# A down-projection written as 44 steps in a fixed order, with reordered first loads and longer distances in the delta rule

## The chip, the cores and the metric

The kernel runs on one core of one Trainium2 chip. The metric is device time in microseconds of one launch. The core's engines, as the profile names them, are TensorE (PE for its matmuls, PEld for its weight loads), VectorE (DVE), ScalarE (ACT), GpSimd (POOL) and SyncE (SP). Each runs its own instructions strictly in order and waits on semaphores of the others. Loads and stores are issued from the queue of one of them: weights from SP, hidden tiles and residual tiles of the down-projection from POOL.

## The reference

One layer over 512 positions of width 2048, in float32. `mem` has 256 tokens, the feed-forward width is 5632.

```python
h = rmsnorm(x, mix_norm)
proj = h @ w_mix_in
y_gdn = gdn_group(proj, ...)         # 8 heads x 128: conv, silu, l2norm, gated delta rule, rmsnorm, gate
y_sc = shortconv_group(proj, ...)    # 1024 channels: gated causal conv of width 3
x = x + concatenate([y_gdn, y_sc]) @ w_mix_out
h = rmsnorm(x, xattn_norm)
mem_n = rmsnorm(mem, mem_norm)
x = x + memory_xattn(h, mem_n, w_xq, w_xk, w_xv, w_xo)
h = rmsnorm(x, ffn_norm)
u = causal_dwconv(h @ w_ffn_up, ffn_conv)
gate, up = u[..., :5632], u[..., 5632:]
x = x + (silu(gate) * up) @ w_ffn_down
return rmsnorm(x, final_norm)
```

In the gated delta rule each head solves, per chunk, a unit triangular system (I + A) with A from the products of its keys, and carries a 128 x 128 state over the chunks; its output goes through an rmsnorm of its own.

## The kernel before

Activations stand transposed: channels on the 128 partitions, the 512 positions along the free axis, so one tile of 128 x 512 holds 128 channels. Matrix products keep float32 accuracy by splitting each operand into a rounded part and a rest (`split` for activations, `wpiece` for weights: ACT makes the rounded part `hi`, DVE subtracts it from the original for `lo`) and by three matmuls for each tile pair (`mm3`: hi times hi, hi times lo, lo times hi). A weight piece is 128 x 1024; it has five buffers for the raw load (`wst`) and three each for `whi` and `wlo`.

The stages in order, by the time at which PE works on them: the key projection of the memory and the two products that follow it (`psk`, `pswk`, to about 304 us), the product of the value side with the output weights (`psmo`, to 404), the q, k, v and z projections of the eight heads (to 851) and the short convolution's (`pssc`, to 1135), the mixer's output (`psx`, to 1309), attention (to 1490), the up-projection (to 2386.6), and the down-projection `psd`, whose last steps run in two halves with the final norm (to 3059.9).

Most code is put in order by a scheduler of the framework. A block under `tc.manual_schedule(engines=...)` keeps the order in which it is written on the engines that it names.

**Down-projection.** Four groups `gq` of four output tiles, each with its PSUM bank (`bank`, eight banks in two pools of five and three, so two groups find room). In a group, 11 steps `c` each bring four hidden tiles (`hid_parts`: load from DRAM on POOL's queue, then `split` into `hdh` and `hdl`) and two weight pieces, for 2 x 2 x 4 x 3 = 48 matmuls of 128 x 512. After a group, each output tile gets the residual tile `x2_d` added (load on POOL, addition on DVE, L865) and its squares summed (`add_squares`: ACT squares, POOL adds to `acc3`, L239; the very first tile's square is written by ACT without an addition). The last group has 10 steps here, no squares at its end, and its eleventh step is the tail in two halves of 256 positions.

**Delta rule.** `delta` is a generator for one head. `weave` and `tick` insert its pieces among the matmuls of the projections: each `yield a, b` ends a piece, adds `a` to a clock that counts PE work, and asks that the next piece come `b` units later. Three matmuls of a projection count 0.65.

**First loads.** The column table `cols` (all norm and convolution weights) is loaded whole on SP, the eight double tiles of `mem` on ACT's queue, and weights follow on SP. `mem_proj` multiplies by `w_xk`, two output tiles in one bank, the first wholly before the second; after the first pair, `mem_norm` sums the squares of `mem` on POOL and multiplies them with `ones` on PE (L230).

Of the kernel before, what the change touches and what calls it, by code (L numbers as in the profile page):

```python
# [25 lines left out]
FC = 4  # L26
EPS = 1e-6
NEG = -1.0e30
B = 32
# [38 lines left out]
def trunk(ctx: ExitStack, tc: tile.TileContext, g):  # L68
# [47 lines left out]
    nc.vector.memset(ones, 1.0)  # L116

# [10 lines left out]
    hgain = cpool.tile([P, 1], F32, tag="hgain", name="hgain")  # L128
    nc.vector.tensor_scalar(hgain, col(C_GAIN), 0.5, None, op0=ALU.mult)

    def wpiece(src):

        st = wp.tile([P, 1024], F32, tag="wst", name=nm("wst"), bufs=5)
# [7 lines left out]
        nc.scalar.copy(hi, st)  # L141
        nc.vector.tensor_tensor(lo, st, f(hi), op=ALU.subtract)  # L142
        return hi, lo
# [99 lines left out]
    mws, m2s = [], []  # L243
    early = {}
    for i in range(KT // 2):
        m2 = T("mem")
        nc.scalar.dma_start(m2.rearrange("p (k m) -> p k m", k=2), g["mem"][2 * i : 2 * i + 2].rearrange("k p m -> p k m"))
        m2s.append(m2)
    with tc.manual_schedule(engines={mybir.EngineType.Activation, mybir.EngineType.DVE, mybir.EngineType.SP}):
        for i in range(KT // 2):  # L250
            if i in (0, 2):
                early[0, i // 2] = wpiece(g["w_xk"][0, i // 2])
            mh, ml = T("mwh", F32R), T("mwl", F32R)
            for k in range(2):
                sl = slice(k * NMEM, (k + 1) * NMEM)
                c = col(C_MEMN + 2 * i + k)
                nc.scalar.activation(mh[:, sl], m2s[i][:, sl], AF.Identity, scale=c)
                nc.vector.scalar_tensor_tensor(ml[:, sl], m2s[i][:, sl], c, f(mh)[:, sl], op0=ALU.mult, op1=ALU.subtract)
                mws.append((mh[:, sl], ml[:, sl]))
# [3 lines left out]
    def mem_norm():  # L263
        for i in range(KT // 2):
            add_squares(macc, m2s[i], i == 0)
# [4 lines left out]
    def mem_proj(w, then=None):  # L270

        out = []
        for n2 in range(KT // 2):
            ps = PM("psk")
            for q in range(2):
                first = [early[0, i] for i in range(2)] if then and n2 == 0 and q == 0 else None
                proj(lambda i: w[2 * n2 + q, i], mws, ps[:, q * NMEM : (q + 1) * NMEM], ready=first)
            if then and n2 == 0:
                then()
            t = T("kt")  # L280
            nc.vector.tensor_tensor(t.rearrange("p (q m) -> p q m", q=2), ps.rearrange("p (q m) -> p q m", q=2), rmem, op=ALU.mult)
            th, tl = T("kth", F32R), T("ktl", F32R)
            nc.scalar.copy(th, t)
            nc.vector.tensor_tensor(tl, t, f(th), op=ALU.subtract)
            for q in range(2):
                out.append((th[:, q * NMEM : (q + 1) * NMEM], tl[:, q * NMEM : (q + 1) * NMEM]))
        return out

    kts = mem_proj(g["w_xk"], mem_norm)
    nc.sync.dma_start(mk, g["masks"])  # L290
    ident = mk[:, M_ID, :]
    idb = cpool.tile([P, CB, B], F32, tag="idb", name="idb")
    nc.sync.dma_start(idb, g["idb"])
# [137 lines left out]
    def delta(h, q, k, v, z):  # L431
# [18 lines left out]
        yield 0.5, 0  # L450
# [13 lines left out]

        psk = PG("pskk")
        four(psk, lambda j: k4[:, j], lambda j: k4[:, j])
        yield 0.9, 0
# [5 lines left out]
        nc.vector.tensor_tensor(dt, psq, dt, op=ALU.mult)  # L473
        at = dt
        yield 0.9, 0
        psv = PG("psvt")
        for j in range(4):
            nc.tensor.transpose(v4(psv)[:, j], v4_[:, j], ident)
        nc.vector.tensor_tensor(v4(v), v4(psv), bc(nk, P), op=ALU.mult)
        yield 0.5, 2.5  # L480
# [31 lines left out]
        yield 0, 9.0  # L512
# [5 lines left out]
        yield 0.5, 1.2  # L518

        for s in (32, 64):  # L520
# [7 lines left out]
            yield 0.5, 1.2  # L528
# [11 lines left out]
            yield 0.7, 1.5  # L540
# [33 lines left out]
        yield 0, 3.0  # L574
        psn = PG("psn")
        nc.tensor.matmul(psn, ones, s1, start=True, stop=True)
# [6 lines left out]
        yield 0.9, 0  # L583
# [168 lines left out]
    def raw(src):  # L752
        t = wp.tile([P, 1024], F32, tag="wst", name=nm("wst"), bufs=5)
# [10 lines left out]
    def sums(s, i):  # L764

        if i == 0:
            return wp.tile([P, 1024], F32, tag="wst", name=nm(s), bufs=5)
# [68 lines left out]
    def hid_parts(c):  # L836
        out = []
        for k in range(FC):
            t = T("hid")
            nc.gpsimd.dma_start(t, hid_d[c * FC + k])  # L840
            out.append(split(t, "hd"))
        return out

# [3 lines left out]
    for gq in range(KT // GN):  # L847
        last = gq == KT // GN - 1
        pss = [bank(gq, q) for q in range(GN)]
        nc_ = NC_ - 1 if last else NC_  # L850
        for c in range(nc_):
            hid = hid_parts(c)
            for n2 in range(GN // 2):
                hi, lo = wpiece(g["w_dn"][c, gq * GN // 2 + n2])
# [105 lines left out]
```

## Time and profile before

| | |
|---|---|
| median of 3 runs | 3063.89 us (3062.74 to 3080.56) |
| the profiled execution | 3061.85 us, span 3059.9 us |
| granted TensorE clock, mean | 0.978 |
| PE busy | 2874.5 us, 94% |
| DVE busy | 1815.5 us, 59% |
| ACT busy | 1339.3 us, 44% |
| POOL busy | 358.4 us, 12% |
| mean DMA rate | 155 GB/s |

Busy time is an average over stages with different limits, so the reading goes by stretches. In a row of a group, the figures after the bar are the busy time and the mean duration of one instruction, then the idle time of that engine just before them and what ended it. In the timeline, a row is a start, a duration and the instruction, with the idle time before it in brackets. A name such as `psd<-hdh,whi` is output from inputs: here the bank of the down-projection from a rounded hidden tile and a rounded weight piece. Matmuls overlap, so their durations don't add up; the distance between starts is what counts. Numbers of the whole program that the page gives are of this one execution.

### The profile page before, as it was taken

How to read it: one execution, taken by the hardware profiler on the slowest of the kernel's cores; microseconds unless marked ns; L12 is line 12 of the kernel's file. 1: busy time of each engine (PE TensorE's matmuls, PEld its weight loads, DVE VectorE, ACT ScalarE, POOL GpSimd, SP SyncE). 2: the span in 40 equal slices, each digit the busy share in tenths (PEclk: the TensorE clock that was granted, in tenths of full speed). 3: DMA queues.
4: the chain of work that ended last, by engine and by line, in shares of the span. 5: the costliest groups of instructions: out<-in, count | busy, mean ns of one | idle time of the engine just before them, and what ended most of it. 6: DMA issues, size and time to landing. Idle time of an engine off the chain costs nothing.

```text
span 3059.9 us, 44141 instructions
## 1 busy us (share of the span) xinstructions
PE 2874.5 (94%) x17521; PEld 2531.8 (83%) x17521; DVE 1815.5 (59%) x2680; ACT 1339.3 (44%) x1879; POOL 358.4 (12%) x438
## 2 busy tenths in 40 slices
PE   7999999999999999999999999999999887878785
PEld 7999788777778888888899999999999665656564
DVE  5445747767753344456788888888888433333334
ACT  5564643443432232245655555555555323323222
POOL 1120000110100001101200000000000203021211
PEclk9999999999999999999999999999999999989898
DMA  6685753333232234455666666666666635354451
GB/s 208 230 287 183 248 156 100 101 84 95 84 100 93 97 127 148 145 180 177 178 175 180 167 170 162 174 179 167 168 164 169 210 111 196 106 173 140 149 162 55
DMA packets 178799, 473.96 MB, mean 155 GB/s; under 512 B 26512, under 2 KB 50464, under 8 KB 178592
## 3 DMA queue, kind: packets, MB, share of 16 engines
q1 hardware_dynamic: 128576, 333.74, 33.0%
q0 software_dynamic: 29984, 102.80, 14.9%
q10 hardware_dynamic: 20032, 34.61, 3.1%
q8 instruction: 137, 2.24, 0.3%
q14 instruction: 70, 0.57, 0.1%
HBM read 427.02 MB, written 44.06 MB: 154 GB/s over the span
## 4 chain that ended last, share of the span: by engine, by line
PE 58%; issue 5%; DVE 3%; ACT 2%; DMA 2%; POOL 1%; DVEq 0%; ACTq 0%; SPq 0%; POOLq 0%
PE px L778 5%; PE px L776 5%; PE px L777 5%; PE psd L153 4%; PE psd L154 4%; PE psd L152 3%; PE pz L776 3%; PE pz L778 3%; PE pz L777 3%; PE pssc L152 3%; PE pssc L154 3%; PE pssc L153 3%; PE psx L153 2%; PE psx L154 2%; PE psx L152 2%
## 5 line engine op out<-in xcount | busy, mean ns | idle before, releaser
L142 DVE TENSOR_TENSOR wlo<-wst,whi 128x1024 fp32r<-128x1024 f32 x408 | 497.7, 1229 | 734.8 <-ACT whi L141 720.8
L141 ACT CAST whi<-wst 128x1024 fp32r<-128x1024 f32 x408 | 424.0, 1049 | 971.2 <-PE psd L153 396.8
L760 ACT CAST whi<-wst 128x1024 fp32r<-128x1024 f32 x176 | 184.5, 1048 | 290.8 <-PE px L777 143.7
L153 PE MATMUL psd<-hdl,whi 128*128 128x512 f32 (+1 forms) x720 | 293.3, 409 | 15.4 <-DVE hdl L148 15.4
L776 PE MATMUL px<-xoh,whi 128*128 128x256 f32 x1056 | 299.6, 284 | 3.6 <-ACT whi L760 3.2
L778 PE MATMUL px<-xoh,wlo 128*128 128x256 f32 x1056 | 299.4, 283 | 0.0
L777 PE MATMUL px<-xol,whi 128*128 128x256 f32 x1056 | 299.3, 283 | 0.0
L152 PE MATMUL psd<-hdh,whi 128*128 128x512 f32 (+1 forms) x720 | 205.4, 399 | 98.6 <-ACT hdh L147 98.5
L154 PE MATMUL psd<-hdh,wlo 128*128 128x512 f32 (+1 forms) x720 | 285.4, 397 | 0.0
L761 DVE TENSOR_TENSOR wlo<-wst,whi 128x1024 fp32r<-128x1024 f32 x176 | 215.3, 1223 | 96.8 <-ACT whi L760 52.0
L152 PEld LDWEIGHTS psd<-hdh,whi 128*128 128x128 f32 x720 | 134.7, 192 | 143.0 <-ACT hdh L147 117.6
L776 PEld LDWEIGHTS px<-xoh,whi 128*128 128x128 f32 x1056 | 203.3, 192 | 4.0 <-ACT whi L760 3.4
L778 PEld LDWEIGHTS px<-xoh,wlo 128*128 128x128 f32 x1056 | 203.4, 193 | 0.0
L777 PEld LDWEIGHTS px<-xol,whi 128*128 128x128 f32 x1056 | 203.3, 193 | 0.0
L778 PE MATMUL pz<-xoh,wlo 128*128 128x256 f32 x704 | 199.3, 283 | 0.9 <-DVE wlo L761 0.9
L776 PE MATMUL pz<-xoh,whi 128*128 128x256 f32 x704 | 199.5, 283 | 0.4 <-ACT whi L760 0.4
L777 PE MATMUL pz<-xol,whi 128*128 128x256 f32 x704 | 199.4, 283 | 0.0
L153 PEld LDWEIGHTS psd<-hdl,whi 128*128 128x128 f32 x720 | 141.9, 197 | 62.6 <-DVE hdl L148 34.8
L760 ACT CAST whi<-s 128x1024 fp32r<-128x1024 f32 x132 | 138.1, 1048 | 86.2 <-PE px L777 60.8
L154 PEld LDWEIGHTS psd<-hdh,wlo 128*128 128x128 f32 x720 | 141.9, 197 | 27.7
L761 DVE TENSOR_TENSOR wlo<-s,whi 128x1024 fp32r<-128x1024 f32 x132 | 161.2, 1223 | 0.6 <-ACT whi L760 0.6
L152 PE MATMUL psq<-hh,whi 128*128 128x512 f32 x384 | 157.8, 411 | 0.0
(306 smaller groups left out, 7363.8 us busy)
## 6 DMA issues: line engine op xcount, KB each, us to landing
wst<-in_w_up SPq DMA_DIRECT2D x132, 512.0 KB, 4.8
wst<-in_w_mix SPq DMA_DIRECT2D x112, 512.0 KB, 3.5
s<-in_w_up POOLq DMA_DIRECT2D x88, 512.0 KB, 6.4
wst<-in_w_dn SPq DMA_DIRECT2D x88, 512.0 KB, 4.3
hid<-hid_d POOLq DMA_DIRECT2D x176, 256.0 KB, 4.2
s<-in_w_up SPq DMA_DIRECT2D x44, 512.0 KB, 4.9
wst<-in_w_xk SPq DMA_DIRECT2D x32, 512.0 KB, 3.5
wst<-in_w_xq SPq DMA_DIRECT2D x32, 512.0 KB, 4.5
```

Source lines behind the costliest of these rows:

```text
L141: nc.scalar.copy(hi, st)
L142: nc.vector.tensor_tensor(lo, st, f(hi), op=ALU.subtract)
L152: nc.tensor.matmul(ps, wh, xh, start=first, stop=False)
L153: nc.tensor.matmul(ps, wh, xl, start=False, stop=False)
L154: nc.tensor.matmul(ps, wl, xh, start=False, stop=last)
L760: nc.scalar.copy(hi, t)
L761: nc.vector.tensor_tensor(lo, t, f(hi), op=ALU.subtract)
L776: nc.tensor.matmul(ps, hi[:, c], xh, start=first and k == 0, stop=False, skip_group_check=True)
L777: nc.tensor.matmul(ps, hi[:, c], xl, start=False, stop=False, skip_group_check=True)
L778: nc.tensor.matmul(ps, lo[:, c], xh, start=False, stop=k == HK - 1, skip_group_check=True)
```

## The change

The down-projection is written as a list of 44 steps (group and `c`). Loads of hidden tiles are asked for two steps ahead, and the parts of hidden tiles and of weight pieces are made two steps and two pieces ahead, on ACT, DVE and POOL in the order written. PE's matmuls of a step stand piece by piece and bank by bank. The tail's parts are made in the same way.

At the start, `cols` is loaded in two portions; the `mem` tiles and four weight pieces come on SP in one written order; the first two output tiles of `mem_proj` are taken together, and the squares of `mem` are used by the norm only after the third pair of output tiles. In `delta`, the products of keys with keys and the transposes are grouped differently, the distances are longer, and the head's norm uses a split operand and two matmuls with rounded ones (`onesr`) where it used one in float32.

```diff
@@ the first loads
-    nc.sync.dma_start(cols, g["cols"])
+    nc.sync.dma_start(cols[:, :C_FFNN], g["cols"][:, :C_FFNN])
...
+        load_mem(0)
+        e0 = raw_piece(g["w_xk"][0, 0])
+        e1 = raw_piece(g["w_xk"][1, 0])
+        for i in (1, 2, 3):
+            load_mem(i)
+        e2 = raw_piece(g["w_xk"][0, 1])
+        e3 = raw_piece(g["w_xk"][1, 1])
+        for i in (4, 5, 6, 7):
+            load_mem(i)
+        nc.sync.dma_start(cols[:, C_FFNN:], g["cols"][:, C_FFNN:])
+        early[0, 0] = parts(e0)
+        mem_parts(0)
+        early[1, 0] = parts(e1)
...
+            if begin and n2 == 0:
+                ps = [PG("psk")[:, :NMEM] for _ in range(2)]
+                for i in range(2):
+                    for k in range(8):
+                        for q in range(2):
+                            hi, lo = early[q, i]
+                            mm3(ps[q], hi[:, k * P : (k + 1) * P], lo[:, k * P : (k + 1) * P], *mws[8 * i + k], i == 0 and k == 0, i == 1 and k == 7)
+                for i in range(1, KT // 2):
+                    add_squares(macc, m2s[i], False)
...
+            if begin and n2 < 2:
+                continue
+            if begin and n2 == 2:
+                mem_norm()
@@ def delta
-        yield 0.5, 0
+        psk = PG("pskk")
+        four(psk, lambda j: k4[:, j], lambda j: k4[:, j])
+        yield 1.4, 1.0
...
-        yield 0, 9.0
+        yield 0, 12.5
...
-        yield 0.5, 1.2
+        yield 0.5, 4.5
...
-            yield 0.5, 1.2
+            yield 0.5, 2.8
...
-            yield 0.7, 1.5
+            yield 0.7, 2.8
...
-        yield 0, 3.0
+        sh, sl = split(s1, "sn")
+        yield 0, 6.0
         psn = PG("psn")
-        nc.tensor.matmul(psn, ones, s1, start=True, stop=True)
+        nc.tensor.matmul(psn, onesr, sh, start=True, stop=False)
+        nc.tensor.matmul(psn, onesr, sl, start=False, stop=True)
@@ the down-projection
+    steps = [(gq, c) for gq in range(KT // GN) for c in range(NC_)]
+    raws, parts_, ws = {}, {}, {}
+
+    def hid_load(i):
+        if i < len(steps):
+            raws[i] = [T("hid") for _ in range(FC)]
+            for k in range(FC):
+                nc.gpsimd.dma_start(raws[i][k], hid_d[steps[i][1] * FC + k])
+
+    def hid_split(i, k):
+        if i < len(steps):
+            parts_.setdefault(i, []).append(split(raws[i][k], "hd"))
+
+    def w_split(p):
+        if p < 2 * len(steps):
+            gq, c = steps[p // 2]
+            ws[p] = wpiece(g["w_dn"][c, gq * GN // 2 + p % 2])
+
+    with tc.manual_schedule(engines={mybir.EngineType.Activation, mybir.EngineType.DVE, mybir.EngineType.Pool}):
+        for i in range(2):
+            hid_load(i)
+        for i in range(2):
+            for k in range(FC):
+                hid_split(i, k)
+            w_split(i)
+        for i, (gq, c) in enumerate(steps):
...
+            hid_load(i + 2)
             for n2 in range(GN // 2):
-                hi, lo = wpiece(g["w_dn"][c, gq * GN // 2 + n2])
+                p = 2 * i + n2
+                w_split(p + 2)
+                for k in range(2):
+                    hid_split(i + 2, 2 * n2 + k)
+                if tail:
+                    continue
+                hi, lo = ws.pop(p)
                 for q in range(2):
                     for k in range(FC):
                         o = k * 2 * P + q * P
-                        mm3(pss[2 * n2 + q], hi[:, o : o + P], lo[:, o : o + P], *hid[k], c == 0 and k == 0, c == nc_ - 1 and k == FC - 1)
+                        mm3(pss[2 * n2 + q], hi[:, o : o + P], lo[:, o : o + P], *parts_[i][k], c == 0 and k == 0, c == nc_ - 1 and k == FC - 1)
```

How the rows on the engines change is shown at three places. The line numbers of the new rows are those of the changed file. First ACT in a middle step of the down-projection, before: `whi` is a rounded weight piece made from a load `wst`, `hdh` a rounded hidden tile made from a load `hid`.

```order
L141 CAST whi_23530<-wst_23528 128x1024
L141 CAST whi_23584<-wst_23582 128x1024
L147 CAST hdh_23476<-hid_23474 128x512
L147 CAST hdh_23482<-hid_23480 128x512
L147 CAST hdh_23488<-hid_23486 128x512
L147 CAST hdh_23494<-hid_23492 128x512
L141 CAST whi_23614<-wst_23612 128x1024
```

And now:

```order
L142 CAST whi_23356<-wst_23354 128x1024
L148 CAST hdh_23360<-hid_23346 128x512
L148 CAST hdh_23364<-hid_23347 128x512
L142 CAST whi_23394<-wst_23392 128x1024
L148 CAST hdh_23398<-hid_23348 128x512
L148 CAST hdh_23402<-hid_23349 128x512
L142 CAST whi_23440<-wst_23438 128x1024
```

Two weight pieces and then four hidden tiles have become one piece and two tiles in turn.

Second PE, in the same stage, before: `psd` are the four banks of a group, `hdl` and `wlo` the rests of the split.

```order
L152 MATMUL psd_23218<-hdh_23650,whi_23668 128x512
L152 MATMUL psd_23219<-hdh_23650,whi_23668 128x512
L152 MATMUL psd_23220<-hdh_23650,whi_23698 128x512
L152 MATMUL psd_23221<-hdh_23650,whi_23698 128x512
L153 MATMUL psd_23218<-hdl_23651,whi_23668 128x512
L154 MATMUL psd_23218<-hdh_23650,wlo_23669 128x512
```

And now, from the second step on:

```order
L153 MATMUL psd_23342<-hdh_23320,whi_23356 128x512
L154 MATMUL psd_23342<-hdl_23321,whi_23356 128x512
L155 MATMUL psd_23342<-hdh_23320,wlo_23357 128x512
L153 MATMUL psd_23342<-hdh_23324,whi_23356 128x512
L154 MATMUL psd_23342<-hdl_23325,whi_23356 128x512
L155 MATMUL psd_23342<-hdh_23324,wlo_23357 128x512
```

Four banks that used both weight pieces (23668 and 23698) for each hidden tile have become one bank and one piece over all hidden tiles.

Third POOL at the second turn between groups, before: `x<-x_d` loads a residual tile, `acc` is the sum of squares, `hid` a hidden tile of a later step.

```order
L864 DMA x_3802_25096<-x_d 128x512
L864 DMA x_3804_25102<-x_d 128x512
L239 TENSOR_TENSOR acc_23217<-acc_23217,sq_25099 128x512
L864 DMA x_3806_25108<-x_d 128x512
L239 TENSOR_TENSOR acc_23217<-acc_23217,sq_25105 128x512
L864 DMA x_3808_25114<-x_d 128x512
L239 TENSOR_TENSOR acc_23217<-acc_23217,sq_25111 128x512
L840 DMA hid_25124<-hid_d 128x512
L239 TENSOR_TENSOR acc_23217<-acc_23217,sq_25117 128x512
```

And now:

```order
L943 DMA x_3849_25220<-x_d 128x512
L240 TENSOR_TENSOR acc_23279<-acc_23279,sq_25223 128x512
L943 DMA x_3851_25226<-x_d 128x512
L240 TENSOR_TENSOR acc_23279<-acc_23279,sq_25229 128x512
L943 DMA x_3853_25232<-x_d 128x512
L240 TENSOR_TENSOR acc_23279<-acc_23279,sq_25235 128x512
L943 DMA x_3855_25238<-x_d 128x512
L240 TENSOR_TENSOR acc_23279<-acc_23279,sq_25241 128x512
L903 DMA hid_25248<-hid_d 128x512
```

Two residual loads stood ahead of the first sum; now each load but the first stands behind the sum of the tile before it, and the hidden loads of the next step behind the last sum.

More of the change, by code (lines that the diff above doesn't have):

```diff
@@ L242, in trunk, with load_mem, raw_piece, parts @@
     macc = cpool.tile([P, S], F32, tag="macc", name="macc")
-    mws, m2s = [], []
+    mws = []
+    m2s = [T("mem") for _ in range(KT // 2)]
+    def load_mem(i):
+        nc.sync.dma_start(m2s[i].rearrange("p (k m) -> p k m", k=2), g["mem"][2 * i : 2 * i + 2].rearrange("k p m -> p k m"))
+    def raw_piece(src):
+        t = wp.tile([P, 1024], F32, tag="wst", name=nm("wst"), bufs=WST)
+        nc.sync.dma_start(t, src)
+        return t
+    def parts(t):
+        hi = wp.tile([P, 1024], F32R, tag="whi", name=nm("whi"))
+        lo = wp.tile([P, 1024], F32R, tag="wlo", name=nm("wlo"))
+        nc.scalar.copy(hi, t)
+        nc.vector.tensor_tensor(lo, t, f(hi), op=ALU.subtract)
+        return hi, lo
@@ new lines, in trunk @@
+        e0 = raw_piece(g["w_xk"][0, 0])
[10 more added lines that the diff above has]
+        early[1, 0] = parts(e1)
+        for i in (1, 2, 3):
+            mem_parts(i)
+        early[0, 1] = parts(e2)
@@ L268, in mem_norm, with mem_proj @@
             nc.vector.tensor_copy(rmem[:, k, :], rmem_t)
-    def mem_proj(w, then=None):
-        out = []
+    def mem_proj(w, begin=False):
+        out, held = [], []
         for n2 in range(KT // 2):
[L274 to L286, printed above, removed]
-        return out
```

113 lines of the change are left out of this document (59 added, 54 removed).

## The prediction

> **What bounds the kernel now.** I read the busy time of each engine by stage first, to see where TensorE (PE) is not kept running. The view of windows gives for each stretch its length, the busy time of PE, its weight loads, DVE, ACT and POOL (instructions in brackets), the granted TensorE clock, the DMA share and GB/s. The four stretches are the qkvz stage with the delta rule woven in, twenty microseconds of it, eleven steps of the down-projection, and one turn between two of its groups.
> ```profile
> 400.00:910.00 510.00, 493.72 (x2628) 395.64 (x2626) 354.20 (x900) 210.63 (x353) 61.45 (x55) 0.99 0.33 97
> 730.00:750.00 20.00, 17.64 (x103) 13.28 (x102) 8.64 (x17) 8.95 (x21) 4.00 (x4) 0.83 0.27 86
> 2555.50:2702.40 146.90, 127.64 (x521) 98.58 (x520) 51.45 (x66) 44.21 (x65) 20.07 (x38) 0.97 0.42 147
> 2702.40:2718.00 15.60, 3.10 (x7) 2.18 (x8) 4.91 (x7) 5.59 (x11) 12.06 (x17) 0.53 0.57 184
> ```
> Eleven steps in 146.9 us are 13.35 us each, and PE is the busiest engine by far; no other engine is near its limit. So the down-projection is PE work with holes. The view of waits, limited to that stage (2389 to 3029 us), says for each engine and line whom it waited for: total, times, longest.
> ```profile
> PE psd L152 <- ACT hdh L147: 98.5, 44, 14.0
> PE psd L153 <- DVE hdl L148: 15.4, 42, 1.3
> ```
> ```profile
> ACT whi L141 <- PE psd L153: 396.8, 42, 10.8
> ```
> PE waits once a step for the rounded hidden parts; ACT waits about as often, for most of a step, until PE lets go of a weight buffer. One step in the timeline (start, duration, engine, line; in brackets the idle time before and what ended it), for ACT, DVE and PE in turn:
> ```profile
> 2458.26 1.99 ACT L141 CAST whi<-wst 128x1024 fp32r<-128x1024 f32 x2 [10.77 <-PE psd L153]
> 2460.16 2.17 ACT L147 CAST hdh<-hid 128x512 fp32r<-128x512 f32 x4
> ```
> ```profile
> 2459.34 2.36 DVE L142 TENSOR_TENSOR wlo<-wst,whi 128x1024 fp32r<-128x1024 f32 x2 [10.07 <-ACT whi L141]
> 2461.62 2.49 DVE L148 TENSOR_TENSOR hdl<-hid,hdh 128x512 fp32r<-128x512 f32 x4
> ```
> ```profile
> 2460.82 1.20 PE L152 MATMUL psd<-hdh,whi 128*128 128x512 f32 x4 [1.47 <-ACT hdh L147]
> ...
> 2464.29 1.07 PE L152 MATMUL psd<-hdh,whi 128*128 128x512 f32 x4
> ...
> 2467.01 1.07 PE L152 MATMUL psd<-hdh,whi 128*128 128x512 f32 x4
> ```
> All preparation of a step queues up in its last microsecond: two weight roundings stand on ACT ahead of the four hidden roundings, and the first of them is released only when PE is nearly through. Twelve matmuls take 2467.01 - 2464.29 = 2.72 us, 0.2267 us each, so 48 are 10.88 us. A step of 13.35 us holds 2.47 us that are no matmul at full pace.
>
> **The down-projection's steps.** PE now finishes the 24 matmuls of one weight piece before it touches the other, and the unit parts for step i+2 are made in step i. ACT needs 1.99 + 2.17 = 4.2 us a step and DVE 2.36 + 2.49 = 4.9 us, against 10.88 us of PE. A weight piece has three buffers, so the rounding of piece p+2 waits for the end of piece p-1 and has two pieces, 10.88 us, until it is needed. I therefore put every wait inside a group at nothing; its cover is that slack, and without it the cost is about the old 1.5 us a step. PE's work is 43 x 48 = 2064 matmuls at 0.2267 us, 467.9 us.
>
> The stage starts later. Its ACT rows stand in a fixed order behind the end of the up-projection, whose last product DVE finishes at 2391.1:
> ```profile
> 2390.45 0.69 DVE L828 TENSOR_TENSOR ucv<-ucv,ucv 128x512 f32<-128x512 f32 x1
> ```
> ```profile
> 2391.17 0.33 ACTq L829 DMA_DIRECT2D hid_d<-ucv  x1
> ```
> From 2391.5, four hidden roundings (2.2 us) and one weight rounding (1.0) put PE's start at 2394.7; the low part comes 1.2 us later, while PE has two matmuls without it (0.8 us of waiting), and the first four microseconds run at half pace after the gap (2 us, from the turn below). The effective start is 2397.5.
>
> A turn between groups adds four output tiles to the residual and sums their squares. The turn of before, first on POOL, then on DVE, then PE's restart:
> ```profile
> 2702.58 1.90 POOL L239 TENSOR_TENSOR acc<-acc,sq 128x512 f32<-128x512 f32 x1 [63.49 <-ACT sq L238]
> 2704.43 0.55 POOL L864 DMA_DIRECT2D x<-x_d  x1
> ...
> 2710.07 1.26 POOL L239 TENSOR_TENSOR acc<-acc,sq 128x512 f32<-128x512 f32 x1 [3.31 <-ACT sq L238]
> ```
> ```profile
> 2700.99 2.36 DVE L142 TENSOR_TENSOR wlo<-wst,whi 128x1024 fp32r<-128x1024 f32 x2 [0.62 <-ACT whi L141]
> 2703.27 0.68 DVE L865 TENSOR_TENSOR x<-psd,x 128x512 f32<-128x512 f32 x1
> 2708.57 0.69 DVE L865 TENSOR_TENSOR x<-psd,x 128x512 f32<-128x512 f32 x1 [4.61 <-DMA x<-x_d]
> ```
> ```profile
> 2714.90 0.79 PE L152 MATMUL psd<-hdh,whi 128*128 128x512 f32 x1 [13.89 <-ACT hdh L147]
> ...
> 2717.07 0.63 PE L153 MATMUL psd<-hdl,whi 128*128 128x512 f32 x1
> 2717.50 0.63 PE L154 MATMUL psd<-hdh,wlo 128*128 128x512 f32 x1
> ```
> A residual load issued at 2704.43 lets DVE add at 2708.57, and the square's sum on POOL ends at 2711.33: 6.9 us from issue to sum. After the wait of 13.9 us matmuls start 0.43 us apart, half pace, at a granted clock of 0.53.
>
> In the new order POOL holds each residual load behind the sum of the tile before it: in the second and third turn load, sum, load, sum, four times. The first load is early. In the group's last step, counted from its start, ACT's second weight rounding follows piece 2i at 5.4 us, and DVE is through its parts and adds the first tile by 9.1 to 9.8; its sum ends at 11.9 and three more rounds of 6.9 us end at 32.6. Behind the last square (31.2) ACT rounds the first weight piece of step i+2, ready at 32.2. PE has step i+1's parts and runs on to 21.8, then waits 10.5 us, 0.8 more for the low part, and loses 2 us to the low clock: 13.3 us. The first turn has one round less, because the very first square is written by ACT: about 6 us. Three turns: 13.3 + 13.3 + 6 = 32.6 us, with 15 more if the hidden loads queued behind on POOL are then late too, and nothing if the loads land ahead. One end of it hangs on the sum on POOL, which took 1.90 us beside DVE's weight subtraction and 1.26 us alone. The Trainium skill, page "SBUF — State Buffer", section "Who interferes with whom", has a DVE operation with two SBUF inputs and a GpSimd operation that reads SBUF block one another on a shared port. By that rule, which these two rows agree with, eleven sums would cost up to 11 x 0.64 = 7 us more if each met such an operation; I take the lone value, since DVE idles in the turn.
>
> The old last group ended here, at the first half-width matmul:
> ```profile
> 3015.50 0.62 PE L152 MATMUL psd<-hdh,whi 128*128 128x256 f32 x3 [0.52 <-ACT hdh L147]
> ```
> The new one comes at 2397.5 + 467.9 + 32.6 = 2898.0, that is 117.5 us earlier; the 0.5 us of waiting goes as well, as the last parts are two steps old.
>
> **The first loads.** PE ends its first 96 matmuls at 27.6 and then waits for the seven sums on POOL; the second fence groups those sums (count, shortest, median and longest ns, first and last start).
> ```profile
> 27.49 0.28 PE L154 MATMUL psk<-mwh,wlo 128*128 128x256 f32 x1
> 32.18 1.22 PE L230 MATMUL psn<-macc,ones 128*128 128x256 f32 x2 [4.41 <-POOL macc L239]
> ```
> ```profile
> L239 POOL TENSOR_TENSOR macc<-macc,sq x7: 1259/1296/2152, 20.2 to 30.9; 128x512 f32<-128x512 f32 x7
> ```
> The change puts 24 more matmuls ahead of that product (24 x 0.12 = 2.9 us of cover for the 4.4 us) and lets PE start with one memory tile. A second load of the column table now stands in the way on ACT. The chain of sums still sets the end: 4 us gained, between 0 and 7.
>
> **The delta rule.** PE's idle time in its window is 510 - 493.72 = 16.3 us. Its waits there (404 to 910 us), and the norm's product:
> ```profile
> PE ps L526 <- ACT bt L517: 7.2, 4, 2.9
> PE psa L515 <- DVE pt L511: 4.5, 3, 1.9
> PE ps L526 <- ACT ww L527: 3.1, 4, 0.9
> PE psn L576 <- POOL s L573: 1.1, 1, 1.1
> ```
> ```profile
> 890.26 1.12 PE L576 MATMUL psn<-s,ones 128*128 128x512 f32 x2
> ```
> Together 15.9 us. The distances grow by more than the longest of these waits (psa 9 to 12.5, psa to ps1 1.2 to 4.5, the others by 1.3 to 3, in units of about a microsecond of PE work), but a head's end is pushed into the next head's start, which shares ACT and DVE. I take three quarters, 12 us, between 0 and 16. The clock of 0.83 over 20 us is 3.4 us of lost pace around one such hole; I take 3 us. The norm's product becomes two single-pass matmuls: 1.12 - 2 x 0.2267 = 0.67 us less, eight times, 5.3 us; the added ACT copy and DVE subtraction per head lie behind qkvz matmuls. The Trainium skill, page "FP8 and Floating Point Precision", section "TensorE Precision Notes", gives true FP32 four passes; four times this trace's pace would be 0.91 us rather than the row's 1.12, and a saving of 3.6 us by that rule.
>
> **Sum.** 117.5 + 0.5 + 4 + 12 + 3 + 5.3 = 142.3 us off the profiled execution's 3061.85: 2919.5. The median of the runs, 3063.89, stands 2.0 us above that execution, so the time against it is 2921.
>
> **Rivals.** *The turns cost nothing*, because the residual loads land early or the next parts are ready: 32.6 us less, 2888. Against it, POOL is in order. Chance 0.05.
>
> *Transfers become the bound, or the turns cost more.* A step moves two weight pieces and four hidden tiles, 2.1 MB; at the 184 GB/s of the turn's window that would take 11.4 us, 0.5 us above PE's 10.9, so 22 us over 43 steps; with 15 us of longer turns 37, 2958. Against it: 184 is what was asked for in that window, not shown as a ceiling. Chance 0.10.
>
> *Half the steady gain stays away*: each of 86 pieces waits 0.75 us for its parts, half the 1.47 us of before, 65 us, 2986. It would need the chain of a piece to miss its slack. Chance 0.06.
>
> *Slower.* If a piece's preparation did not overlap the pieces before it, because a buffer is let go one piece late, each piece would add rounding and subtracting of one weight piece and two hidden tiles, (4.2 + 4.9) / 2 = 4.5 us, to its 5.44: 86 x 4.5 = 387 us more, 3308. It decides from (142.3 + 30.6) / 86 = 2.0 us a piece on. For it: the fixed order lets one late operation hold all behind it. Against it: in before, ACT's rounding starts while PE still works on the last matmuls. Chance 0.03, with 0.01 for a time near the old one. That PE's order does not change is no rival, since the listing of its rows shows that it does.
>
> The forecast keeps 0.75. One per cent, 31 us, is about what a measurement of this kernel can tell from no change; faster by more than that 0.96, within it 0.01, slower 0.03. The range goes from the seamless turns to the longer ones with slower transfers, 2888 to 2958; the terms of the first loads and of the delta rule at their bounds (3 us and 11 us better, 4 us and 20 us worse) lie inside.
>
> **What will show it.** Right: steps 10.9 us apart; PE waits of at least 10 us at the second and third turn, ended by ACT's weight rounding, with POOL alternating loads and sums 6.9 us apart; first full-width matmul of the stage near 2394.7 less what was gained before it; chain waits in the delta window under 5 us. Wrong: waits for whi or hdl within a group, steps above 11.3 us, or a low clock inside the steps.

## The result, and the profile after

The changed kernel takes 2925.74 us in the median of four runs (2924.16 to 2928.81), the kernel before 3065.43 us in its four. The ratio of the means is 0.9536, with a 95% interval of 0.9503 to 0.9568. The profiled execution has a span of 2925.0 us, 134.9 us less than before.

Where the 134.9 us went is read from the starts of PE's first product of each stage in the two traces:

| stretch | before, us | after, us | difference | forecast |
|---|---|---|---|---|
| start to the heads' first product | 404.2 | 403.9 | -0.3 | -4 |
| from there to the mixer's output (delta rule woven in) | 731.6 | 727.3 | -4.3 | -20.3 |
| from there to the last product of the up-projection | 1250.5 | 1251.2 | +0.7 | 0 |
| from there to the first half-width matmul | 629.2 | 501.4 | -127.8 | -117.5 |
| the tail | 44.4 | 41.2 | -3.2 | -0.5 |

So the total came out right, while four of its parts were off, by 2.7 to 16 us. The windows of the changed kernel (columns as in the prediction), for the delta stretch, most of the second group's steps, the turn behind them, and the tail:

```profile
403.90:1131.20 727.30, 713.20 (x3658) 580.16 (x3657) 427.65 (x991) 273.30 (x431) 62.98 (x57) 0.99 0.32 98
2536.00:2640.00 104.00, 104.00 (x461) 86.11 (x460) 48.92 (x62) 41.32 (x62) 18.41 (x34) 1.00 0.57 196
2640.00:2656.00 16.00, 9.13 (x35) 6.75 (x34) 2.92 (x3) 3.64 (x6) 6.78 (x9) 0.77 0.17 42
2883.80:2925.00 41.20, 15.30 (x106) 13.30 (x104) 22.38 (x37) 11.94 (x21) 14.72 (x18) 0.71 0.30 103
```

Inside a group PE is busy without a break, at full clock, while 196 GB/s come in. What is left are the start of the stage and the turns; in the second turn PE is busy for 9.13 of 16 us and the clock falls. PE's waits in the down-projection, 2381 to 2900 us:

```profile
PE psd L153 <- ACT whi L142: 21.9, 4, 7.8
PE psd L155 <- DVE wlo L143: 1.2, 4, 0.4
```

Against 113.9 us of waits for hdh and hdl before, 23.1 us stand, and 14.0 of the 21.9 are the three turns. POOL in the second turn, and PE's restart after it:

```profile
2634.97 1.29 POOL L240 TENSOR_TENSOR acc<-acc,sq 128x512 f32<-128x512 f32 x1 [33.16 <-ACT sq L239]
2636.20 0.56 POOL L943 DMA_DIRECT2D x<-x_d  x1
2640.79 1.28 POOL L240 TENSOR_TENSOR acc<-acc,sq 128x512 f32<-128x512 f32 x1 [4.03 <-ACT sq L239]
```

```profile
2653.14 0.79 PE L153 MATMUL psd<-hdh,whi 128*128 128x512 f32 x1 [6.52 <-ACT whi L142]
```

Loads and sums alternate as forecast, one round every 5.8 us. In the tail DVE is busy for 22.38 us, where the same stretch of before had 26.92, as the tail's weight and hidden parts now lie ahead of it. The tail is 3.2 us shorter.

In the first stage PE now starts at 7.45 us instead of 10.22, but the wait for the norm of the memory grew. PE, and ACT shortly before:

```profile
34.31 1.22 PE L231 MATMUL psn<-macc,ones 128*128 128x256 f32 x2 [7.57 <-POOL macc L240]
```

```profile
16.47 0.21 ACT L429 ACTIVATE na<-cols 128x8 f32<-128x8 f32 x1 [1.93 <-DMA cols<-in_cols]
```

The norm's product stands at 34.31 us instead of 32.18. `na` is the exponential of the heads' decay constants, which the scheduler put among the memory's parts on ACT; it reads the second portion of the column table, and the squares behind it wait with it.

In the delta stretch PE waits for these (403 to 960 us), and the longest of them shows on ACT:

```profile
PE ps L579 <- ACT bt L570: 4.7, 1, 4.7
PE ps L579 <- DVE bt L590: 3.8, 2, 2.5
PE psn L630 <- ACT snh L148: 2.1, 3, 0.8
```

```profile
623.50 0.20 ACT L517 ACTIVATE nk<-ss 128x4 f32<-128x4 f32 x1 [2.35 <-DVE ss L512]
623.73 1.28 ACT L518 ACT_TABLE_LOAD   x1
625.02 0.21 ACT L518 ACTIVATE nk<-nk 128x4 f32<-128x4 f32 x1
625.13 0.57 ACT L570 COPY bt<-psa 128x512 f32<-128x512 f32 x1
```

The copy `bt` of one head stands behind the key norm `nk` of the next, with a table load between: the meeting that the prediction named as a risk of the longer distances. The prediction's sign, chain waits under 5 us, did not come: these three are 10.6 us.

### The profile page after: what moved, and what is told of

Read it like the earlier page. It is cut to its first block, busy times and chain, and to the rows that moved or that the text cites. A ratio compares the mean times of both kernels' runs of the same rounds, so it can differ in the third digit from the quotient of the medians.

```text
span 2925.0 us, 44163 instructions
## 1 busy us (share of the span) xinstructions
PE 2832.6 (97%) x17521; PEld 2524.7 (86%) x17521; DVE 1820.2 (62%) x2707; ACT 1346.5 (46%) x1887; POOL 354.7 (12%) x438
## 4 chain that ended last, share of the span: by engine, by line
PE 58%; issue 8%; DVE 3%; DMA 2%; ACT 1%; POOL 1%; ACTq 0%; SPq 0%; DVEq 0%; POOLq 0%
PE px L833 6%; PE px L831 6%; PE px L832 6%; PE psd L155 3%; PE pz L831 3%; PE pz L833 3%; PE pz L832 3%; PE psd L153 3%; PE psd L154 3%; PE pssc L153 3%; PE pssc L155 3%; PE pssc L154 3%; PE psx L154 2%; PE psx L155 2%; PE psx L153 2%
## 5 line engine op out<-in xcount | busy, mean ns | idle before, releaser
L153 PE MATMUL psd<-hdh,whi 128*128 128x512 f32 (+1 forms) x720 | 280.4, 389 | 21.9 <-ACT whi L142 21.9
L154 PE MATMUL psd<-hdl,whi 128*128 128x512 f32 (+1 forms) x720 | 279.6, 388 | 0.0
```

The source lines that it names most:

```text
L153: nc.tensor.matmul(ps, wh, xh, start=first, stop=False)
L154: nc.tensor.matmul(ps, wh, xl, start=False, stop=False)
```

## Experiments

**One part at a time.** Each of the three parts of the change was put on the old kernel alone, and a fourth kernel changes POOL's order at the turns. For the first three the edit is a part of the diff above: the down-projection; all of `delta` with `onesr`; the first loads with `mem_proj`.

> The old kernel with the new down-projection alone. Theory A (the stage's gain stands by itself): the stretch from the last matmul of the up-projection to the end falls from 673.5 us to about 542.5 us as it does in the changed kernel, so 131 us off: 2931 us on a profile, about 2934 in the median; the waits of PE in the stage are the four of the changed kernel (start about 8 us, turns about 1.3, 6.5 and 6.2). Theory B (the predicted terms: the stage gives 118 us and the other two parts the rest): 2944 us.

Measured: 2933.16 us, ratio 0.9565 (0.9543 to 0.9587). From the last product of the up-projection to the end of the span 542.8 us, waits for whi 22.0 us in four. Theory A holds: the stage's gain stands by itself, 131 us of the 135.

> The old kernel with the new delta rule alone (grouping, distances, split norm). Theory A (what the changed kernel's stage times say: qkvz and short-convolution stages together 727.3 us against 731.6): 4 us off, about 3060; a wait of several us at one head's psa or ps1 product, where it meets the next head's start on ACT, is to be seen. Theory B (the predicted term): 20 us off, about 3044, chain waits in the stage under 5 us in sum.

Measured: 3059.44 us, ratio 0.9979 (0.9968 to 0.9990); the stretch is 729.1 us, with the same wait of 4.7 us for `bt`. Theory A. The whole delta change is worth some 4 us, not 20.

> The old kernel with the new first loads alone. Theory A (the chain of squares on ACT and sums on POOL sets the end of the wait, and the wait of ACT for the second portion of the column table puts that chain 2 us later): PE starts near 7.5 us, the norm's product of the memory near 34.3 us instead of 32.2, and the whole is about 1 us slower, 3064. Theory B (the predicted term): 4 us faster, 3060.

Measured: 3064.07 us, ratio 0.9999 (0.9985 to 1.0012). PE starts at 7.2 us, waits 7.5 us for the sums, and ACT waits 1.94 us at `na`. The first product of the heads comes at 402.1 us; over the kernels with the old first loads it came at 404.2, 405.4 and 405.5, with the new ones at 402.1 to 403.9. So the part gives perhaps 2 us in its stage, below what the whole time can tell. The mechanism is theory A's; the microsecond that it should have lost is not shown, and neither are the 4 us of theory B.

> The changed kernel with the four residual loads of a group issued on POOL ahead of the first sum of squares. Theory A (the stall at a turn is the round of load, addition, square and sum that POOL's order makes): no wait over 1 us at the three turns, the 14.0 us of waits for whi and 1.1 us for wlo there go, and some 5 us of low clock with them; about 2906 us. Theory B (the loads of hidden tiles behind the sums are late next, or the first weight rounding is late for another reason): the waits stay within 3 us of the old ones or move to hdh, 2920 to 2925.

```diff
+                x2s_ = [T("x3") for _ in range(GN)]
                 for q in range(GN):
+                    nc.gpsimd.dma_start(x2s_[q], x2_d[gq * GN + q])
+                for q in range(GN):
                     n = gq * GN + q
-                    x2 = T("x3")
-                    nc.gpsimd.dma_start(x2, x2_d[n])
+                    x2 = x2s_[q]
                     nc.vector.tensor_tensor(x2, pss[q], x2, op=ALU.add)
```

Measured: 2905.84 us, ratio 0.9474 (0.9452 to 0.9497). PE's waits in the stage, and POOL in the second turn:

```profile
PE psd L153 <- ACT whi L142: 7.8, 1, 7.8
```

```profile
2632.37 6.27 POOL L240 TENSOR_TENSOR acc<-acc,sq 128x512 f32<-128x512 f32 x4 [31.58 <-ACT sq L239]
2638.59 1.61 POOL L903 DMA_DIRECT2D hid<-hid_d  x3
```

Only the start's wait for `whi` is left; the four sums run one after the other. The stage from its last up-projection product to its last matmul fell from 514.3 to 491.8 us, so the turns had cost 22.5 us in all. Theory A.

**Which half of the down-projection's change gives the gain.** One kernel keeps the parts two steps ahead but lets PE take four banks and both weight pieces for each hidden tile again. Another takes away one buffer of the weight parts, which makes their release one piece late. Each of the two has one execution.

> The changed kernel with the parts made ahead as in the change, but PE again taking all four banks and both weight pieces for each hidden tile. Theory A (the lead of the parts gives most, the order of PE the rest, through the release of weight buffers): the rounding of a step's second weight piece waits for the end of the step before, is ready 1.1 us later, its low part 2.4 us later, while PE needs them 1.4 and 1.8 us after its start; so about 0.6 us of wait a step on wlo, steps of 11.5 us, 25 us slower than the changed kernel. Theory B (the order of PE is the whole gain): steps of 13.3 us as before, 100 us slower. Theory C (the lead is the whole gain): 10.9 us, no slower.

```diff
+            held_ = []
...
-                for q in range(2):
-                    for k in range(FC):
-                        o = k * 2 * P + q * P
-                        mm3(pss[2 * n2 + q], hi[:, o : o + P], lo[:, o : o + P], *parts_[i][k], c == 0 and k == 0, c == nc_ - 1 and k == FC - 1)
+                held_.append((hi, lo))
+            if not tail:
+                for k in range(FC):
+                    for q in range(GN):
+                        hi, lo = held_[q // 2]
+                        o = k * 2 * P + (q % 2) * P
+                        mm3(pss[q], hi[:, o : o + P], lo[:, o : o + P], *parts_[i][k], c == 0 and k == 0, c == nc_ - 1 and k == FC - 1)
```

> The changed kernel with two instead of three buffers for the rounded weight piece and for its low part, in all stages; only the down-projection is read. The rounding of piece p+2 then waits for the end of piece p. Theory A (a piece of 5.44 us covers 2.3 us of preparation, so even a release one piece later costs nothing): steps of 10.9 us, no PE wait inside a group. Theory B (the slower rival of the prediction, a buffer let go one piece late): 4.5 us more a piece, steps near 20 us.

```diff
-        hi = wp.tile([P, 1024], F32R, tag="whi", name=nm("whi"))
-        lo = wp.tile([P, 1024], F32R, tag="wlo", name=nm("wlo"))
+        hi = wp.tile([P, 1024], F32R, tag="whi", name=nm("whi"), bufs=2)
+        lo = wp.tile([P, 1024], F32R, tag="wlo", name=nm("wlo"), bufs=2)
...
```

The second edit stands at two more places that make weight parts.

Measured: 2943.1 us for the first; its stage, from the last up-projection product to the last matmul, is 532.7 us against 514.3 of the changed kernel and 643.0 of before. A hundred microseconds within its second group, its waits of the stage, and ACT ahead of its second turn:

```profile
2540.00:2640.00 100.00, 100.00 (x443) 82.83 (x442) 44.09 (x56) 38.68 (x57) 15.00 (x29) 1.00 0.55 189
```

```profile
PE psd L153 <- ACT whi L142: 37.3, 6, 10.9
```

```profile
2637.74 1.05 ACT L142 CAST whi<-wst 128x1024 fp32r<-128x1024 f32 x1 [6.80 <-PE psd L154]
```

The second, 2976.84 us with its other stages slower too, has the same: 530.6 us for the stage, full within a group, with its long waits at the start and the turns.

```profile
2575.00:2675.00 100.00, 100.00 (x443) 82.84 (x442) 44.00 (x55) 38.43 (x55) 15.46 (x29) 1.00 0.56 192
```

```profile
PE psd L153 <- ACT whi L142: 37.7, 4, 11.7
```

In these windows neither waits: there theory C of the first and theory A of the second hold, and the 0.6 us a step that I had expected did not show. Both lose 16 to 18 us, at the turns. The second weight rounding of a group's last step now waits until about that step's end, half a step (5.44 us) later, and the chain of additions, squares and sums that stands behind it on DVE and ACT starts as much later, three times. So of the 129 us of the stage the lead of the parts, with the written order on ACT, DVE and POOL that makes it, gives some 110, and the order of PE with the early release the rest, by way of the turns. The lead and the written order were not taken apart. The slower rival, a release one piece late, costs nothing per piece.

**The first loads.** The next kernel squares each memory tile right behind its parts.

> The changed kernel with each memory tile squared on ACT right behind its parts, so that POOL can begin to sum some 10 us earlier. Theory A (the chain of squares and sums sets the end of the first wait): the norm's product near 27 us instead of 34.3, its wait of 7.6 us under 2, the low clock behind it gone; 8 to 10 us faster, about 2917. Theory B (the squares only push the parts back on ACT, and PE waits for those): the waits move to the parts, and the time stays within 2 us of the changed kernel.

```diff
                 mws.append((mh[:, sl], ml[:, sl]))
+        add_squares(macc, m2s[i], i == 0)
...
-        add_squares(macc, m2s[0], True)
...
-                for i in range(1, KT // 2):
-                    add_squares(macc, m2s[i], False)
```

Measured: 2925.14 us, ratio 0.9540 (0.9524 to 0.9556), no different from the changed kernel; the heads start at 401.3 us instead of 403.9. The wait for the sums is gone, also because the scheduler now puts the norm's product behind 288 matmuls instead of 120, at 56.64 us; so the 27 us of theory A were not tried. PE waits for the parts instead: 10.9 us for `mwh` where it had 7.5. ACT shows why:

```profile
9.21 0.91 ACT L267 ACTIVATE mwh<-mem,cols 128x256 fp32r<-128x256 f32 x2
16.61 0.21 ACT L427 ACTIVATE na<-cols 128x8 f32<-128x8 f32 x1 [6.49 <-DMA cols<-in_cols]
```

Nearer to theory B, by another cause: the scheduler now puts `na` ahead of the second tile's square, and ACT stands there 6.49 us until the column table has come.

**The delta rule's edits.** Grouping, distances and the split norm were taken apart. The first kernel has the old distances alone put back.

> The changed kernel with the old distances of the delta rule (9.0, 1.2, 1.2, 1.5 and 3.0 in place of 12.5, 4.5, 2.8, 2.8 and 6.0); the split norm and the new grouping stay. The stretch from the first product of the heads' projections to the mixer's output took 731.6 us before and 727.3 after. Theory A (the split norm gives 5.3 us and the distances nothing, as they trade waits at one place for waits at another): 725 to 728 us here, total within 3 us of the changed kernel. Theory B (the longer distances save some 12 us, and the new grouping costs as much): 735 us or more here, total 8 us slower or more.

```diff
-        yield 0, 12.5
+        yield 0, 9.0
...
-        yield 0.5, 4.5
+        yield 0.5, 1.2
...
-            yield 0.5, 2.8
+            yield 0.5, 1.2
...
-            yield 0.7, 2.8
+            yield 0.7, 1.5
...
-        yield 0, 6.0
+        yield 0, 3.0
```

Measured: 2942.27 us, ratio 0.9594 (0.9572 to 0.9617), stretch 740.6 us. Theory B: beside the other edits the longer distances do save 13 us, and something else in the delta change costs as much. I put it on the grouping, and the next three kernels tested that. They stand on the kernel with the loads ahead of the sums. In all three `na` is written behind the memory's parts; the first and third also have the early squares.

> The changed kernel with the residual loads ahead of the sums, with each memory tile squared right behind its parts and the exponential of the decay constants moved behind those on ACT, and with the old grouping of the delta rule's first products (transposes, keys with keys, keys with queries, transposes, a piece each) under the new distances; split norm as in the change. Read by stages. First loads, up to the first product of the heads' projections (403.9 us in the changed kernel, 401.3 with the squares early): Theory A (the early squares failed because ACT stood 6.5 us at the decay constants, waiting for the second portion of the column table): the norm's product near 27 us without a wait, the stage 394 to 397. Theory B: 400 or more. Delta rule, from there to the mixer's output (727.3 us): Theory A (the new grouping costs some 15 us and the new distances win them back): 715 us or less. Theory B (the grouping costs only with the old distances): 725 to 730.

> As the run before in the turns; the delta rule with old grouping and old distances, so that only the split norm is left of its change; the exponential of the decay constants behind the parts on ACT, squares where the change has them. First loads: Theory A (the change's 1.9 us of ACT waiting for the column table pass on to the sums): the norm's product near 32.4 us, the stage 401 to 402; Theory B: 403 to 404. Delta rule: Theory A (the split norm alone is worth 5.3 us of 731): 724 to 727 us, which is as good as the whole change; Theory B (its extra copy and subtraction on ACT and DVE cost what PE saves): 730 or more.

> The same as the first of these with the new grouping, and with 16.0 in place of 12.5 ahead of the transposes psa. Delta rule: Theory A (the 4.7 us wait of the changed kernel is a meeting with the next head's start on ACT and goes when psa comes after it; 8 us of low clock hang on it and on a second one): 715 to 721 us. Theory B (a later psa only moves the meeting): 726 us or more.

The new edit of the first on the delta rule, in excerpts; the second has it too, with the old distances of the kernel above:

```diff
-        psk = PG("pskk")
-        four(psk, lambda j: k4[:, j], lambda j: k4[:, j])
-        yield 1.4, 1.0
+        yield 0.5, 0
...
+        psk = PG("pskk")
+        four(psk, lambda j: k4[:, j], lambda j: k4[:, j])
+        yield 0.9, 0
...
+        yield 0.9, 0
         psv = PG("psvt")
...
-        yield 1.4, 2.5
+        yield 0.5, 2.5
```

Measured, in order: 2896.79 us (ratio 0.9449, 0.9427 to 0.9471), 2922.45 (0.9537, 0.9510 to 0.9564), 2915.81 (0.9510, 0.9488 to 0.9533). The delta stretch took 726.8, 744.4 and 747.0 us. The first is theory B: with the new distances the old grouping changes nothing. With the old ones it changes little (744.4 against 740.6). The second is theory B by its number, but not by its reason, which was that the split costs what PE saves. Only the split norm is left there of the delta change, and the stretch is 13.7 us longer than 730.6 and 730.8, which the kernels with the old delta rule have. The third is theory B: a still later psa only meets something else (its largest waits are 13.4 us for `psn` behind `dt` on DVE).

In the first loads, PE waits no more for the sums where the squares are early and `na` late; the norm's product again stands behind 288 matmuls, at 52.23 and 50.26 us. The heads start at 400.0 and 400.2 us, which is theory B by a hair (and at 397.3 in the next kernel, whose first loads are the same), and PE now waits 3.6 to 3.8 us for the memory's low parts on DVE. Moving `na` alone (the second kernel) left the norm's product at 33.48 us and the heads' start at 405.6: theory B, or worse.

So the split norm was the suspect, and the last kernel takes it out where the distances are long.

> The kernel oldgroup_newdist with the head's norm again as one float32 product, without the split of its operand. Its delta stretch (first product of the heads' projections to the mixer's output) took 726.8 us with the split. With the old distances the split made that stretch longer (744.4 us with it, 730.6 and 730.8 in the two kernels that keep the old delta rule whole). Theory A (at the new distances the split is worth what PE saves, 5.3 us): 732 us, total about 2902. Theory B (the split's copy and subtraction cost here as they did with the old distances): 715 us or less, total about 2884.

```diff
-        sh, sl = split(s1, "sn")
...
-        nc.tensor.matmul(psn, onesr, sh, start=True, stop=False)
-        nc.tensor.matmul(psn, onesr, sl, start=False, stop=True)
+        nc.tensor.matmul(psn, ones, s1, start=True, stop=True)
...
-        yield 0.5, 0
+        yield 0.9, 0
```

Measured: 2885.58 us, ratio 0.9413 (0.9397 to 0.9430), the best kernel of this study. Its delta stretch, and below it that of the kernel with the split:

```profile
397.30:1113.20 715.90, 709.44 (x3659) 578.16 (x3658) 424.97 (x983) 268.31 (x424) 62.88 (x57) 1.00 0.33 100
```

```profile
400.00:1126.80 726.80, 711.58 (x3658) 579.04 (x3657) 424.93 (x991) 273.38 (x431) 64.37 (x57) 0.99 0.32 98
```

Theory B, 0.9 us outside its bound: 10.9 us less without the split. PE idles 6.5 us instead of 15.2 and the clock is full. What the split adds shows in ACT's waits with it:

```profile
ACT snh L148 <- POOL s L626: 13.0, 8, 2.3
```

Without the split, PE's product reads POOL's sum of squares itself. With it, ACT has to round that sum first, and stands 13.0 us in eight heads until POOL has made it, with all later work of ACT queued behind. That the waits of other work come from there is what the lines suggest; the runs show only that the split as a whole, with the shorter cost in its last `yield`, lengthens the stretch, by 13.7 us at the old distances and 10.9 at the new.

## Why the prediction was right, and where it was not

*Steps of the down-projection.* I put the waits inside a group at nothing, with the parts' slack as cover. The runs show this mechanism: 104.00 busy of 104.00 us, and the cover held even with one buffer less. The forecast of 0.2267 us a matmul held as well.

*The start of the stage.* Forecast at 2394.7 less what was gained before it. PE's last up-projection matmul came 3.9 us earlier, and the stage began at 2390.6, 4.1 earlier than the forecast.

*The turns.* The mechanism was right (load, addition, square, sum, in POOL's order, ended by ACT's weight rounding), and `turn_fix` shows it. The term was mis-sized: 32.6 us forecast, 22.5 shown, and the forecast that the second and third turn wait at least 10 us was wrong (6.5 and 6.2). The failed step is the round of 6.9 us, read from a turn of before in which weights and a second residual load moved beside the load (282 GB/s while it was under way). In the new turn nothing else moved (85 GB/s), a load issued at 2636.20 lets DVE add at 2639.27, 3.1 us instead of 4.1, and a round takes 5.8. Eight rounds that are 1.1 us shorter make 8.8 of the 10 us by which the stage did better than forecast. That the load is faster because it is alone fits these figures; no run varied it.

*First loads.* 4 us forecast, 0.3 shown between these two traces, perhaps 2 over all kernels. I had written that the chain of sums still sets the end, and that a second load of the column table stands in the way on ACT; the failed step is to have given the 2.9 us of added cover without charging the later start of that chain (22.09 us on POOL instead of 20.22), which took it back. Moving `na` away gave back 0.8 us of the 2.1 by which the norm's product came later; what else delays the chain stays open.

*The delta rule.* 20.3 us forecast, 4.3 shown. The distances stood at 15 us, 12 of waits and 3 of clock. Without the split they bring that, and in that way: 730.6 us with the old ones, in the kernel with the new down-projection alone, and 715.9 with the new ones, in the last kernel. PE idles 17.2 us in the first and 6.5 in the second. (What else differs there is the grouping, which changed nothing with the split norm, and edits outside the stretch.) With the split they bring 13.3 us in one pair of kernels (740.6 to 727.3) and 17.6 in the other (744.4 to 726.8), but PE's idle time falls by only 4.8 and 5.0 us, and the larger part is the clock, from 0.97 to 0.99. There the agreement with 15 is luck. The stretch of the first kernel and of the two with old distances and the split:

```profile
405.40:1136.00 730.60, 713.38 (x3658) 578.37 (x3657) 427.57 (x983) 268.90 (x423) 64.21 (x57) 0.99 0.32 98
403.60:1144.20 740.60, 721.68 (x3659) 586.43 (x3658) 433.46 (x991) 273.07 (x431) 65.89 (x57) 0.97 0.32 97
405.60:1150.00 744.40, 724.24 (x3659) 588.50 (x3658) 431.06 (x991) 272.88 (x431) 64.91 (x57) 0.97 0.32 96
```

The grouping, which I left at nothing, is at nothing within 4 us. The failed step is the norm: "the added ACT copy and DVE subtraction per head lie behind qkvz matmuls". PE's saving is there, but the 5.3 us were misread: the 1.12 us are a duration that runs into the next matmul. By starts, in the old kernel and then in the changed one:

```profile
944.54 1.02 PE L576 MATMUL psn<-s,ones 128*128 128x512 f32 x2
945.00 0.79 PE L152 MATMUL pssc<-hh,whi 128*128 128x512 f32 x1
945.62 0.39 PE L153 MATMUL pssc<-hl,whi 128*128 128x512 f32 x1
```

```profile
955.28 0.39 PE L630 MATMUL psn<-snh,onesr 128*128 128x512 f32 x1
955.51 0.39 PE L631 MATMUL psn<-snl,onesr 128*128 128x512 f32 x1
955.74 0.40 PE L153 MATMUL pssc<-hh,whi 128*128 128x512 f32 x1
```

The float32 product and one matmul of 0.23 us take 1.08 us from start to start, which leaves 0.85 us for the product; the two new ones take 0.46. That is an estimated 0.4 us a head and 3 us in all, near the prediction's other price of 3.6. But the split made the stretch 11 to 14 us longer, where I had booked a gain of 5.3. I had priced its operations by their time and not by what they wait for: one engine more in the chain, with a queue behind it.

*The sum.* 2921 forecast and 2925.74 measured: 10 us too little for the down-projection, 3 too little for the tail, and some 20 too much for the other two parts. The close total is in part luck, these errors cancelling. The delta rule's bound of 11 us better does not follow from the terms that the prediction gives. Of the rivals, transfers as the bound and half the gain are refuted by the full windows; the seamless turns are not what the change does, but what a small edit of it does.

## What to carry to other kernels

When a step is prepared ahead in a fixed order, look at the places where the order changes: loads that stand behind arithmetic on the same queue make a chain of round trips, and issuing them first took 20 us here. An operation added to an engine that has room by its busy time still has a place in that engine's queue; ask what it waits for and who stands behind it, since the split norm saved PE some 3 us and still made the time 11 to 14 us longer. And read a forecast's parts against the stages, not its total against the time.

## What the runs showed of the hardware that I had not expected

The low clock does not need a long gap. In the kernel with the old grouping and distances under the split norm, one head's small products came after waits of 1.1 and 1.0 us. PE at both, and then windows of 2.5 us (after the length comes PE's busy time; the clock is third from the end):

```profile
807.39 0.43 PE L581 MATMUL ps<-bt,nt 32*32 32x32 f32 x8 [1.11 <-ACT bt L572]
809.71 0.34 PE L581 MATMUL ps<-bt,nt 32*32 32x32 f32 x5 [0.99 <-ACT ww L582]
```

```profile
797.50:800.00 2.50, 1.31 (x8) 0.82 (x6) 0.19 (x1) 0.00 (x0) 0.00 (x0) 1.00 0.39 66
800.00:802.50 2.50, 1.85 (x11) 1.64 (x12) 1.55 (x5) 0.92 (x2) 0.00 (x0) 1.00 0.43 170
802.50:805.00 2.50, 2.50 (x13) 2.08 (x12) 0.00 (x0) 2.48 (x11) 2.17 (x2) 1.00 0.00 0
805.00:807.50 2.50, 1.39 (x9) 0.85 (x8) 2.11 (x5) 1.82 (x4) 1.83 (x3) 1.00 0.00 0
807.50:810.00 2.50, 1.51 (x23) 0.99 (x23) 2.46 (x7) 2.12 (x4) 0.00 (x0) 1.00 0.22 33
810.00:812.50 2.50, 2.50 (x33) 1.94 (x27) 1.73 (x4) 0.26 (x1) 0.00 (x0) 0.61 0.45 177
812.50:815.00 2.50, 2.50 (x12) 1.74 (x11) 1.02 (x4) 1.79 (x3) 0.00 (x0) 0.50 0.20 32
815.00:817.50 2.50, 2.50 (x7) 1.92 (x7) 1.21 (x1) 0.23 (x1) 0.00 (x0) 0.52 0.12 24
```

PE was busy for 2.90 of the 5 us from 805 on, and the clock fell to half for about 7 us. In the 5 us from 797.50 on it was busy for 3.16, with one wait of 1.84 us, and the clock stayed at 1.00. Over the whole delta stretch the mean clock was 0.97 in this kernel and 1.00 in the best one. The Trainium skill, page "TensorE: Matmul & The Clock Gate", section "HAM oscillation — how this bites in real kernels", puts the danger at gaps in PE's work of more than about 3.4 us. This trace differs: two gaps of a third of that, some 2 us apart, came before a fall, while the wait of 1.5 us, and a short one of 0.3 behind it, in each old step of the down-projection left the clock at 0.97 on average over eleven steps. Which share of busy time decides, and whether the small products of 32 x 32 between the gaps count like large ones, was not tried.
